# A two-layer model block on one core: experts taken in pairs in the column halves of TensorE, weights loaded in runs of 8 KB

## The chip, the core and the metric

The kernel runs on one core of one Trainium2 chip. A core has TensorE (PE in the profile, with PEld for its weight loads), VectorE (DVE), ScalarE (ACT), GpSimd (POOL) and SyncE (SP, whose queue starts nearly all DMA transfers of this kernel). The metric is the device time of one execution in microseconds; lower is better. Several executions are timed and the median is taken.

## What is computed

Two layers over 256 tokens of width 1024, each a mixer (retention and RWKV7), a cross-attention over a memory, and a grouped mixture of experts, with a layer norm behind each. The change touches the experts alone:

```python
def grouped_moe(x, router_w, router_bias, w_gate, w_up, w_down):
    ...
    y = jnp.zeros_like(t)
    for e in range(N_EXPERTS):
        h = jax.nn.silu(t @ w_gate[e]) * (t @ w_up[e])
        y = y + combine[:, e:e + 1] * (h @ w_down[e])
    return y.reshape(B, S, D)
```

There are 16 experts of width 512 in 4 groups; a token takes two experts of one group, so `combine` is zero for the other 14. Everything is fp32.

## The kernel before

**Which tokens an expert sees.** Each expert has a list of up to 64 tokens (`CAP`). `gather` (L1191) builds, for one group of four experts, the one-hot matrix `oh` of token against place in the list, and `columns` (L1199) multiplies the tokens with it: `xs` (the tokens as a high and a low part, tokens on the partitions, 1024 features in the row) is the operand that is loaded into the array as weights, 128 features at a time, and `oh` is streamed through with 256 columns. The result `xe` has features on the partitions and the 64 places of four experts in its columns. A layer has 128 such products. `columns` is a generator that `moe` moves on a step at a time between the products of the experts.

**The experts.** `moe` (L1106) goes through pairs of experts `p`. For each of the two experts, `expert_in` (L1238) makes the gate product, later the up product: the 64 columns of `xe` are the weights, a piece of the expert's matrix is streamed with 512 columns. 64 columns fill half of the array's 128 columns, so the even 128-row blocks of the contraction run in one column half and the odd ones in the other, side by side. The two partial sums then stand in different partitions of PSUM, and `halves` (L1249) adds them: ACT copies one half across (L1253, `low`), DVE adds the other (L1254). Silu is on ACT (L1150), the product of gate and up on DVE. `expert_mid` (L1256) transposes the result of both experts (four transposes, L131, in which `act` is the operand loaded as weights and the identity is streamed) and copies it from PSUM (`hT`, L1262). `expert_out` (L1265) makes the down product in the same way as the others, again with `halves` (`y`). `weighed` (L1276) multiplies with the combine weights and splits into `yh` (ACT, L1283) and `yl` (DVE, L1284), and `combine` (L1288) adds both to the output sums with eight full-width products (`y<-yh,ohT` and `y<-yl,ohT`), one pair later.

All products go through `mm`, so all of them have line L127 in the profile. One fp32 product of 64 columns by 512 is two instructions of the trace (written 128*64 there: 128 rows, 64 columns). The two column halves take instructions side by side when neighbours in PE's order lie in different halves.

**The weights.** 96 pieces of 1 MB a layer. `take` (L150 is the line of `fetch` that starts the transfer) asks for a piece on SP's queue and puts it into the next slot of a ring of 18 slots, which are buffers of several pools (`raw`, `wh`, `x`, `A` in the profile). A transfer waits until PE is through with the piece that had the slot before. `piece` (in the printed lines) gives a piece of 128 rows by k: each partition gets rows of the matrix that lie 128 rows apart, so runs of 2 KB in memory for gate and up (512 columns) and of 4 KB for down (1024 columns).

**What sets the order.** The code is written in the order of `moe`, and a scheduler orders each engine's instructions from it by when operands are ready and buffers come free; `behind` holds instructions back. PE runs its instructions strictly in the order that results.

Of the kernel before, what the change touches and what calls it, by code (L numbers as in the profile page):

```python
# [9 lines left out]
F32 = mybir.dt.float32  # L10
# [3 lines left out]
AF = mybir.ActivationFunctionType  # L14
# [6 lines left out]
D = 1024  # L21
# [4 lines left out]
FE = 512  # L26
# [89 lines left out]
class Build:  # L116
# [66 lines left out]
    @staticmethod  # L183
    def piece(w, k0, nk, c0, n):
        return w.rearrange("(k p) c -> p k c", p=128)[:, k0:k0 + nk, c0:c0 + n], [128, nk, n]

    @staticmethod
    def finish(steps):
# [917 lines left out]
    def moe(self, l, x, mem):  # L1106
        tc, nc, a, c = self.tc, self.nc, self.a, self.c
        wg, wu, wd = a["moe_w_gate"][l], a["moe_w_up"][l], a["moe_w_down"][l]
        py = [[self.pp.tile([128, 512], F32, name="y", tag="a", bufs=2) for _ in range(2)]]
        with ExitStack() as ctx:  # L1110
            mo = ctx.enter_context(tc.tile_pool(name="moe", bufs=1))
            with tc.tile_pool(name="route", bufs=1) as rp:
                rx = []
                for k in range(0, DK, 2):
                    ps = self.pp.tile([128, 2, 2, 128], F32, name="g", tag="b", bufs=4)
                    for j in range(2):
                        for tb in range(2):
# [12 lines left out]
            py.append([self.pp.tile([128, 512], F32, name="y", tag="c", bufs=2) for _ in range(2)])  # L1130
            for tb in range(2):
                for jc in range(2):
                    for i in range(2):
                        self.mm(py[tb][jc], self.identr, xs[i][:, tb, jc * 512:jc * 512 + 512], i == 0, False)
            lists, acts, ys = {}, {}, {}
            step = self.gather(mo, 0, xs, rank, cws, lists)
            self.finish(step)

            for p in range(NP + 2):
                if p < NP:  # L1140
                    if p % 2 == 0 and p < NP - 2:
                        step = self.gather(mo, p // 2 + 1, xs, rank, cws, lists)
                    xe = lists[p // 2][0]
                    act = mo.tile([128, 512], F32, name="act", bufs=2)
                    for o in range(2):
                        with self.behind(self.onehot) if p == 0 and o == 0 and NM > 0 else ExitStack():
                            ps = self.expert_in(wg[2 * p + o], [t[:, :, 2 * (p % 2) + o] for t in xe])
                        self.halves(mo, ps, act, o)
                        next(step, None)
                    nc.scalar.activation(act, act, AF.Silu)  # L1150
                    acts[p] = act
                if 1 <= p <= NP:
                    hT = self.expert_mid(mo, acts.pop(p - 1))
                if p < NP:
                    if p >= 2:
                        self.combine(p - 2, ys.pop(p - 2), lists[(p - 2) // 2][1][:, p % 2], py)
                    us = self.aux.tile([128, 512], F32, name="us", tag="sg", bufs=3)
                    for o in range(2):
                        ps = self.expert_in(wu[2 * p + o], [t[:, :, 2 * (p % 2) + o] for t in xe])
                        self.halves(mo, ps, us, o)  # L1160
                        next(step, None)
                    nc.vector.tensor_mul(out=act, in0=act, in1=us)
                    if p % 2:
                        self.finish(step)
                if 1 <= p <= NP:
                    y = [self.aux.tile([128, 512], F32, name="y", tag="sg", bufs=3) for _ in range(2)]
                    for o in range(2):
                        self.expert_out(mo, wd[2 * p - 2 + o], hT, y, o)
                        if p == NP and o == 0:
                            self.combine(p - 2, ys.pop(p - 2), lists[(p - 2) // 2][1][:, p % 2], py)  # L1170
                    ys[p - 1] = self.weighed(mo, y, lists[(p - 1) // 2][2][:, (p - 1) % 2:(p - 1) % 2 + 1])
                if p == NP + 1:
                    self.combine(p - 2, ys.pop(p - 2), lists[(p - 2) // 2][1][:, p % 2], py)
        self.extra.close()
        self.ring = [r for r in self.ring if r[1] == "raw2"]
        gb = self.norm(a["ln3_g"][l], a["ln3_b"][l])
        self.ring = [(self.wpool, "raw", self.nraw)] * self.nraw
        if l + 1 < self.layers:
            w = a["xa_wkv"][l + 1]
            self.prefetch([self.piece(w, hf * 4, 4, D + 512, 512) for hf in range(2)])  # L1180
        n = nc.values_load(flag[0:1, 0:1], min_val=0, max_val=2 * S)
        with tc.If(n > 0):
            self.overflow(l, xs, py, cover)
        x = self.xp.tile([128, 2, D], F32, name="x")

        self.layer_norm(lambda tb, j: py[tb][j], gb, x, LN_EPS / ALPHA ** 2)
        self.tail.close()
        self.tap("ln3", x)
        return x

    def gather(self, mo, g, xs, rank, cws, lists):  # L1191
# [5 lines left out]
        xe = []  # L1197

        def columns(k0):  # L1199
            t = mo.tile([128, 2, 4, 64], F32, name="xe", tag="xe", bufs=NXE)  # L1200
            ps = self.pp.tile([128, 2, 4, 64], F32, name="g", tag="b", bufs=4)
            for j in range(2):
                for i in range(2):
                    for tb in range(2):
                        k = k0 + j
                        self.mm(ps[:, j], xs[i][:, tb, k * 128:k * 128 + 128], oh[:, tb], j == 0 and tb == 0 and i == 0, tb == 1 and i == 1)
            if k0 % 4:
                nc.vector.tensor_copy(out=flat(t), in_=flat(ps))
            else:
                nc.scalar.copy(out=flat(t), in_=flat(ps))  # L1210
            xe.append(t)
# [23 lines left out]
            columns(k)  # L1235
        lists[g] = xe, ohT, ws

    def expert_in(self, w, xe):  # L1238

        ps = self.pp.tile([128, 512], F32, name="g", tag="b", bufs=4)  # L1240
        for hf in range(2):
            raw = self.take(*self.piece(w, hf * 4, 4, 0, FE))
            for k in range(0, 4, 2):
                t = xe[hf * 2 + k // 2]
                for j in range(2):
                    self.mm(ps[j * 64:j * 64 + 64, :], t[:, j], raw[:, k + j, :], hf == 0 and k == 0, hf == 1 and k == 2)
        return ps

    def halves(self, mo, ps, out, o):  # L1249

        h, x = slice(o * 64, o * 64 + 64), slice(64 - o * 64, 128 - o * 64)
        low = mo.tile([128, 512], F32, name="low", bufs=1)
        self.nc.scalar.copy(out=low[h], in_=ps[x])  # L1253
        self.nc.vector.tensor_add(out=out[h], in0=ps[h], in1=low[h])  # L1254

    def expert_mid(self, mo, g):  # L1256

        ps = self.pp.tile([128, 4, 128], F32, name="g", tag="b", bufs=4)
        for f in range(4):
            self.tr(ps[:, f, :], g[:, f * 128:f * 128 + 128])  # L1260
        hT = mo.tile([128, 4, 128], F32, name="hT", bufs=1)
        self.nc.vector.tensor_copy(out=flat(hT), in_=flat(ps))  # L1262
        return hT

    def expert_out(self, mo, wd, hT, y, o):  # L1265

        pd = [self.pp.tile([128, 512], F32, name="g", tag="b", bufs=4) for _ in range(2)]
        for hf in range(2):
            raw = self.take(*self.piece(wd, hf * 2, 2, 0, D))
            for jc in range(2):  # L1270
                for j in range(2):
                    self.mm(pd[jc][j * 64:j * 64 + 64, :], hT[:, hf * 2 + j, o * 64:o * 64 + 64], raw[:, j, jc * 512:jc * 512 + 512], hf == 0, hf == 1)
        for jc in range(2):
            self.halves(mo, pd[jc], y[jc], o)

    def weighed(self, mo, y, ws):  # L1276

# [94 lines left out]
```

## Time and profile before

| | |
|---|---|
| runs timed | 1318.68, 1309.84 and 1310.9 us, median 1310.9 |
| profiled execution | 1307.25 us, span 1305.5, granted clock 0.970 |
| PE | busy 1199.3 us, 92% of the span |
| DVE | busy 769.7 us, 59% |
| ACT | busy 500.1 us, 38% |
| DMA | 331.08 MB, 254 GB/s in the mean |

The share of an engine is its busy time over the whole span, which has stages of different kinds. A stage is read from the windows; a wait says which instruction was held up and by whom; the timeline gives start and length of instructions of one kind that stand behind each other. The expert stages lie at 451.4 to 675 us (layer 0) and 1073 to 1296 us (layer 1).

### The profile page before, as it was taken

To read this page: it belongs to the slowest core of one execution; us is meant where nothing else is said; L and a number is where in the kernel's file an instruction comes from. 1 tells how busy PE (TensorE), PEld (TensorE's weight loads), DVE (VectorE), ACT (ScalarE), POOL (GpSimd) and SP (SyncE) were. 2 spreads that over 40 slices of the span, in tenths; PEclk is the share of its full clock that TensorE was granted. 3 is DMA by queue.
4 is the path that set the end of the run, shared out by engine and by line. 5 is a ranking of instruction groups with operands and counts; after the bars stand their busy time and mean duration, and the time that the engine had idled before them with its cause. 6 is when DMAs were issued, how large, how long until landed. Compare 5 with 4: busy or idle time off the path is not lost. (4 is left out here: it accounts for less than half of the span.)

```text
span 1305.5 us, 19592 instructions
## 1 busy us (share of the span) xinstructions
PE 1199.3 (92%) x7648; PEld 850.1 (65%) x7648; DVE 769.7 (59%) x1574; ACT 500.1 (38%) x817; POOL 81.9 (6%) x157
## 2 busy tenths in 40 slices
PE   8999998998999999999969999989979969999995
PEld 7886787996988734433339876879959754433331
DVE  6589787777548423323356797876875562342335
ACT  4566433453544322322235664234534222232222
POOL 0022322000000000000000113220000000000000
PEclk9999989999999999999989999899989979999997
DMA  9746222298635899999986453131987249999994
GB/s 321 264 142 192 78 76 76 79 373 283 233 129 205 315 396 402 399 396 401 400 335 224 153 181 106 43 108 66 348 291 285 108 166 389 401 396 400 402 397 188
DMA packets 189842, 331.08 MB, mean 254 GB/s; under 512 B 23152, under 2 KB 80880, under 8 KB 188720
## 3 DMA queue, kind: packets, MB, share of 16 engines
q1 hardware_dynamic: 187728, 324.51, 69.0%
q10 hardware_dynamic: 1728, 3.15, 0.7%
q0 software_dynamic: 288, 2.10, 0.4%
q8 instruction: 64, 1.05, 0.3%
q14 instruction: 34, 0.28, 0.1%
HBM read 321.86 MB, written 7.87 MB: 253 GB/s over the span
## 5 line engine op out<-in xcount | busy, mean ns | idle before, releaser
L136 DVE TENSOR_TENSOR wh<-raw,wh 128x1024 fp32r<-128x1024 f32 (+1 forms) x204 | 233.3, 1147 | 122.8 <-ACT wh L135 121.4
L135 ACT CAST wh<-raw 128x1024 fp32r<-128x1024 f32 (+1 forms) x204 | 199.9, 981 | 181.8 <-PE acc L127 167.7
L127 PE MATMUL acc<-xT,wh 128*128 128x256 f32 x1824 | 246.0, 290 | 2.1 <-DVE xT L136 1.3
L127 PEld LDWEIGHTS acc<-xT,wh 128*128 128x128 f32 x1824 | 228.5, 193 | 6.5 <-issue 2.1
L1253 ACT COPY low<-g 64x512 f32<-64x512 f32 x128 | 74.2, 580 | 289.5 <-PE g L127 263.6
L127 PE MATMUL g<-raw,xe 128*64 128x512 f32 x688 | 157.7, 598 | 4.5 <-DVE hT L1262 3.5
L127 PEld LDWEIGHTS g<-raw,xe 128*64 128x64 f32 x688 | 46.0, 136 | 90.7 <-issue 80.2
L127 PE MATMUL acc<-wh,xT 128*128 128x512 f32 x384 | 99.8, 405 | 2.7 <-DVE vg L557 2.7
L1254 DVE TENSOR_TENSOR y<-g,low 64x512 f32<-64x512 f32 x64 | 44.1, 688 | 77.4 <-ACT low L1253 77.3
L127 PE MATMUL g<-raw,hT 128*64 128x512 f32 x352 | 81.4, 596 | 5.5 <-DVE y L1254 2.7
L127 PEld LDWEIGHTS acc<-wh,xT 128*128 128x128 f32 x384 | 70.2, 188 | 19.6 <-DVE vg L557 3.5
L1254 DVE TENSOR_TENSOR us<-g,low 64x512 f32<-64x512 f32 x32 | 22.0, 688 | 94.4 <-ACT low L1253 94.3
L1254 DVE TENSOR_TENSOR act<-g,low 64x512 f32<-64x512 f32 x32 | 22.0, 688 | 75.1 <-ACT low L1253 75.0
L127 PEld LDWEIGHTS g<-raw,hT 128*64 128x64 f32 x352 | 26.0, 137 | 55.0 <-issue 41.9
L127 PE MATMUL acc<-wh,memT 128*128 128x512 f32 x192 | 50.7, 415 | 0.3 <-ACT memT L135 0.3
L127 PE MATMUL acc<-memT,wh 128*128 128x256 f32 x384 | 46.7, 283 | 1.1 <-DVE wh L136 0.7
L127 PEld LDWEIGHTS acc<-memT,wh 128*128 128x128 f32 x384 | 46.1, 190 | 1.8 <-DVE wh L136 0.9
L127 PE MATMUL acc<-wh,mT 128*128 128x512 f32 x192 | 45.9, 397 | 0.7 <-DVE xr L406 0.7
L127 PE MATMUL acc<-wh,oT 128*128 128x512 f32 x192 | 45.6, 394 | 1.0 <-DVE x L406 0.8
L127 PE MATMUL acc<-ys,wh 128*128 128x256 f32 x384 | 45.6, 280 | 0.0
L127 PEld LDWEIGHTS acc<-ys,wh 128*128 128x128 f32 x384 | 45.4, 188 | 0.0
L127 PEld LDWEIGHTS g<-oh,xs 128*128 128x128 f32 x256 | 33.5, 196 | 17.1 <-issue 11.2
(296 smaller groups left out, 1684.5 us busy)
## 6 DMA issues: line engine op xcount, KB each, us to landing
raw<-in_w_in_dram SPq DMA_DIRECT2D x46, 1024.0 KB, 5.2
raw<-in_moe_w_down_dram SPq DMA_DIRECT2D x44, 1024.0 KB, 14.9
raw<-in_moe_w_gate_dram SPq DMA_DIRECT2D x43, 1024.0 KB, 14.0
raw<-in_moe_w_up_dram SPq DMA_DIRECT2D x43, 1024.0 KB, 13.8
raw<-in_xa_wkv_dram SPq DMA_DIRECT2D x16, 1024.0 KB, 10.1
wh<-in_moe_w_up_dram SPq DMA_DIRECT2D x15, 1024.0 KB, 14.2
A<-in_moe_w_down_dram SPq DMA_DIRECT2D x10, 1024.0 KB, 13.7
A<-in_moe_w_gate_dram SPq DMA_DIRECT2D x9, 1024.0 KB, 13.7
```

The source lines that it names most:

```text
L127: self.nc.tensor.matmul(out, lhsT, rhs, start=start, stop=stop, skip_group_check=True)
L135: self.nc.scalar.copy(out=hi, in_=src)
L136: (eng or self.nc.vector).tensor_sub(out=lo, in0=src, in1=hi)
L1253: self.nc.scalar.copy(out=low[h], in_=ps[x])
L1254: self.nc.vector.tensor_add(out=out[h], in0=ps[h], in1=low[h])
```

## The change

The two experts of a pair take the two column halves, instead of the even and odd blocks of one expert. Each half then holds a finished sum, so `halves` is no longer there; Silu, the product of gate and up, and `weighed` read the sums from PSUM. `expert_in` and `expert_out` become `experts_in` and `experts_out`, which take a piece of each of the two experts and alternate between them.

A piece now holds the same megabyte in another shape: `together` gives each partition rows that lie next to each other, 8 KB in one run, four rows of gate and up or two of down. So partition p holds rows 4p to 4p+3 of a half of the matrix (2p and 2p+1 for down), and the other operand must have its contraction in the same order: `columns` loads `xs` into the array with a step of four columns, `expert_mid` loads `act` with a step of two. The number of products, transposes, transfers and their bytes, and the order of pieces and slots on SP's queue, are the same.

```diff
+    def together(w, hf):
+        n = w.shape[0] // 256
+        return w.rearrange("(h p k) c -> h p k c", h=2, k=n)[hf], [128, n, w.shape[1]]
...
+                    with self.behind(self.onehot) if p == 0 and NM > 0 else ExitStack():
+                        ps = self.experts_in(wg, p, xe)
                     act = mo.tile([128, 512], F32, name="act", bufs=2)
-                    for o in range(2):
-                        with self.behind(self.onehot) if p == 0 and o == 0 and NM > 0 else ExitStack():
-                            ps = self.expert_in(wg[2 * p + o], [t[:, :, 2 * (p % 2) + o] for t in xe])
-                        self.halves(mo, ps, act, o)
-                        next(step, None)
-                    nc.scalar.activation(act, act, AF.Silu)
+                    nc.scalar.activation(act, ps, AF.Silu)
...
-                        self.mm(ps[:, j], xs[i][:, tb, k * 128:k * 128 + 128], oh[:, tb], j == 0 and tb == 0 and i == 0, tb == 1 and i == 1)
+                        c0 = k // 4 * 512
+                        self.mm(ps[:, j], xs[i][:, tb, c0 + k % 4:c0 + 512:4], oh[:, tb], j == 0 and tb == 0 and i == 0, tb == 1 and i == 1)
...
+    def experts_in(self, w, p, xe):
         ps = self.pp.tile([128, 512], F32, name="g", tag="b", bufs=4)
         for hf in range(2):
+            raw = [self.take(*self.together(w[2 * p + o], hf)) for o in range(2)]
+            for k in range(4):
                 t = xe[hf * 2 + k // 2]
+                for o in range(2):
+                    self.mm(ps[o * 64:o * 64 + 64, :], t[:, k % 2, 2 * (p % 2) + o], raw[o][:, k, :], hf == 0 and k == 0, hf == 1 and k == 3)
...
-    def halves(self, mo, ps, out, o):
-        h, x = slice(o * 64, o * 64 + 64), slice(64 - o * 64, 128 - o * 64)
-        low = mo.tile([128, 512], F32, name="low", bufs=1)
-        self.nc.scalar.copy(out=low[h], in_=ps[x])
-        self.nc.vector.tensor_add(out=out[h], in0=ps[h], in1=low[h])
...
-            self.tr(ps[:, f, :], g[:, f * 128:f * 128 + 128])
+            c0 = f // 2 * 256
+            self.tr(ps[:, f, :], g[:, c0 + f % 2:c0 + 256:2])
...
+    def experts_out(self, wd, p, hT):
         pd = [self.pp.tile([128, 512], F32, name="g", tag="b", bufs=4) for _ in range(2)]
         for hf in range(2):
+            raw = [self.take(*self.together(wd[2 * p + o], hf)) for o in range(2)]
             for jc in range(2):
                 for j in range(2):
+                    for o in range(2):
+                        self.mm(pd[jc][o * 64:o * 64 + 64, :], hT[:, hf * 2 + j, o * 64:o * 64 + 64], raw[o][:, j, jc * 512:jc * 512 + 512],
+                                hf == 0 and j == 0, hf == 1 and j == 1)
```

The gathers move on at other places too: both steps of a pair's gate come behind it, and both of an even pair's up.

PE's order changes with it. The first place is a late pair of layer 0, from its down products to the next pair's gate. Before (`raw`, `wh`, `x` and `A` are weight pieces; the rows with `hT` are down products, those with `xe` gate or up products, `g<-cst,act` the transposes, `y<-...` the products of `combine`):

```order
L127 MATMUL g<-raw,hT 64x512 x4
L127 MATMUL g<-raw_5526,hT 64x512 x4
L127 MATMUL g<-wh,hT 64x512 x8
L127 MATMUL g<-wh,xe 64x512 x4
L127 MATMUL y<-yh,ohT 128x512
L127 MATMUL y<-yl,ohT 128x512
...
L127 MATMUL g<-x,xe 64x512 x4
L127 MATMUL y<-yl,ohT 128x512
L127 MATMUL g<-A,xe 64x512 x4
L131 MATMUL g<-cst,act 128x128 x4
L127 MATMUL g<-A,xe 64x512 x4
```

The same place in the change, where `raw` and `raw_5366` are the pieces of the pair's two experts, each in its own column half:

```order
L127 MATMUL g<-raw,hT 64x512 x2
L127 MATMUL g<-raw_5366,hT 64x512
L127 MATMUL g<-raw,hT 64x512
L127 MATMUL g<-raw_5366,hT 64x512 x2
L127 MATMUL g<-raw,hT 64x512
L127 MATMUL g<-raw_5366,hT 64x512
L127 MATMUL g<-wh,hT 64x512 x8
L127 MATMUL y<-yh,ohT 128x512 x2
L127 MATMUL y<-yl,ohT 128x512 x2
L127 MATMUL y<-yh,ohT 128x512
L127 MATMUL g<-wh,xe 64x512
L131 MATMUL g<-cst,act 128x128 x4
```

The down products went from four of one expert after four of the other to two, one, one, two, one, one; combine stands directly behind them; and a single gate product stands ahead of the four transposes, where a group of four stood.

The second place is ACT's order in the middle of layer 0 (`low` is the copy of a half, `act<-` Silu, `yh` the weighing, `xe<-g` a copy of the gather). Before:

```order
L1210 COPY xe<-g 128x512
L1253 COPY low<-g 64x512 x2
L1150 ACTIVATE act<-act 128x512
L1253 COPY low<-g 64x512 x6
L1283 ACTIVATE yh<-y,ws 128x512 x2
```

In the change:

```order
L1153 ACTIVATE act<-g 128x512
L1216 COPY xe<-g 128x512
L1284 ACTIVATE yh<-g,ws 128x512 x2
L1153 ACTIVATE act<-g 128x512
L1227 CAST ohT<-g 128x512
```

The eight copies of a pair are no longer there, and Silu and the weighing take `g`, a bank of PSUM, as their operand.

## Rows read from the trace of the kernel before

**Rows 1.** The page's 40 slices: busy tenths of the DMA engines.

```profile
DMA  9746222298635899999986453131987249999994
```

**Rows 2.** Windows: length, busy us of PE PEld DVE ACT POOL, clock, DMA share, GB/s.

```profile
451.40:675.00 223.60, 212.07 (x1021) 83.23 (x1020) 77.18 (x113) 63.26 (x101) 0.00 (x0) 0.99 1.02 394
1073.00:1296.00 223.00, 210.71 (x1021) 82.73 (x1020) 78.38 (x119) 60.25 (x98) 0.00 (x0) 0.99 0.97 372
1060.00:1100.00 40.00, 35.14 (x210) 19.27 (x211) 12.56 (x38) 8.11 (x14) 0.00 (x0) 0.91 0.79 293
```

**Rows 3.** PE's waits at 451.4 to 675 us: total us, times, longest.

```profile
PE g L127 <- DVE hT L1262: 3.4, 4, 1.3
PE g L127 <- DVE y L1254: 3.0, 6, 0.5
PE y L127 <- ACT yh L1283: 2.4, 3, 2.0
PE y L127 <- DVE yl L1284: 0.6, 2, 0.3
...
PE g L127 <- DMA raw<-in_moe_w_down_dram: 0.2, 1, 0.2
```

**Rows 4.** Waits of SP's DMA queue at 400 to 720 us.

```profile
SPq L150 <- PE g L127: 119.9, 62, 7.9
```

**Rows 5.** PE's waits at 1073 to 1296 us, where they differ from rows 3.

```profile
PE g L127 <- DVE y L1254: 2.5, 5, 0.5
```

**Rows 6.** Timeline of PE: start us, us, engine, line, op, tiles, shape, count.

```profile
451.42 3.65 PE L127 MATMUL g<-raw,xe 128*64 128x512 f32 x16
...
471.57 1.03 PE L127 MATMUL g<-raw,xe 128*64 128x512 f32 x4
472.53 2.15 PE L127 MATMUL g<-oh,xs 128*128 128x256 f32 x16
474.62 2.79 PE L127 MATMUL g<-raw,xe 128*64 128x512 f32 x12
...
513.20 3.94 PE L127 MATMUL g<-raw,hT 128*64 128x512 f32 x16
517.67 4.18 PE L127 MATMUL g<-wh,hT 128*64 128x512 f32 x16 [0.53 <-DVE y L1254]
...
615.94 1.03 PE L127 MATMUL g<-A,xe 128*64 128x512 f32 x4
616.80 7.04 PE L127 MATMUL g<-raw,xe 128*64 128x512 f32 x32
623.66 7.04 PE L127 MATMUL g<-raw,hT 128*64 128x512 f32 x32
```

**Rows 7.** Timeline of PE behind the last down product of layer 0.

```profile
670.05 1.14 PE L127 MATMUL y<-yh,ohT 128*128 128x512 f32 x2 [1.96 <-ACT yh L1283]
```

**Rows 8.** Groups by line and shape, ACT: busy us, mean ns, idle before.

```profile
L1283 ACT ACTIVATE yh<-y,ws 128x512 fp32r<-128x512 f32 x32 | 23.1, 722 | 0.7
```

**Rows 9.** Groups by line and shape, PE's weight loads, 440 to 660 us.

```profile
L127 PEld LDWEIGHTS g<-oh,xs 128*128 128x128 f32 x128 | 16.1, 188 | 8.6 <-issue 6.0 <-DVE yl L1284 0.8 <-DVE ws L1231 0.8
```

**Rows 10.** Groups by line and shape, DVE in the mixer, whole span.

```profile
L812 DVE TENSOR_TENSOR blkT<-blkO,blkM 64x225 f32<-64x225 f32 x4 | 2.1, 534 | 0.1
...
L814 DVE TENSOR_REDUCE blkO<-blkT 64x15 f32<-64x225 f32 x4 | 1.5, 374 | 0.1
...
L812 DVE TENSOR_TENSOR blkT<-blkO,blkM 64x64 f32<-64x64 f32 x4 | 1.0, 255 | 0.1
...
L814 DVE TENSOR_REDUCE blkO<-blkT 64x8 f32<-64x64 f32 x4 | 0.8, 212 | 0.1
```

**Rows 11.** Windows by the runs that move: 2 KB, 4 KB, mixed with 8 KB.

```profile
624.00:642.00 18.00, 17.47 (x80) 6.18 (x78) 7.00 (x10) 5.03 (x9) 0.00 (x0) 1.00 1.05 389
1228.00:1240.00 12.00, 11.47 (x50) 4.30 (x50) 4.09 (x6) 3.07 (x5) 0.00 (x0) 1.00 1.03 416
...
692.80:695.40 2.60, 2.60 (x17) 2.18 (x16) 2.24 (x5) 1.51 (x3) 0.00 (x0) 1.00 1.01 353
```

More of the change, by code (lines that the diff above doesn't have):

```diff
@@ L185, in piece @@
         return w.rearrange("(k p) c -> p k c", p=128)[:, k0:k0 + nk, c0:c0 + n], [128, nk, n]
+    @staticmethod
+    def together(w, hf):
+        n = w.shape[0] // 256
+        return w.rearrange("(h p k) c -> h p k c", h=2, k=n)[hf], [128, n, w.shape[1]]
     @staticmethod
@@ L1143, in moe @@
                     xe = lists[p // 2][0]
+                    with self.behind(self.onehot) if p == 0 and NM > 0 else ExitStack():
+                        ps = self.experts_in(wg, p, xe)
                     act = mo.tile([128, 512], F32, name="act", bufs=2)
-                    for o in range(2):
-                        with self.behind(self.onehot) if p == 0 and o == 0 and NM > 0 else ExitStack():
-                            ps = self.expert_in(wg[2 * p + o], [t[:, :, 2 * (p % 2) + o] for t in xe])
-                        self.halves(mo, ps, act, o)
-                        next(step, None)
-                    nc.scalar.activation(act, act, AF.Silu)
+                    nc.scalar.activation(act, ps, AF.Silu)
                     acts[p] = act
+                    if p % 2 == 0:
+                        for _ in range(2):
+                            next(step, None)
                 if 1 <= p <= NP:
@@ L1156, in moe @@
                         self.combine(p - 2, ys.pop(p - 2), lists[(p - 2) // 2][1][:, p % 2], py)
[L1157 to L1162, printed above, removed]
+                    ps = self.experts_in(wu, p, xe)
+                    nc.vector.tensor_mul(out=act, in0=act, in1=ps)
                     if p % 2:
                         self.finish(step)
+                    else:
+                        for _ in range(2):
+                            next(step, None)
                 if 1 <= p <= NP:
[L1166 to L1171, printed above, removed]
+                    pd = self.experts_out(wd, p - 1, hT)
+                    if p == NP:
+                        self.combine(p - 2, ys.pop(p - 2), lists[(p - 2) // 2][1][:, p % 2], py)
+                    ys[p - 1] = self.weighed(mo, pd, lists[(p - 1) // 2][2][:, (p - 1) % 2:(p - 1) % 2 + 1])
                 if p == NP + 1:
@@ L1236, in gather @@
         lists[g] = xe, ohT, ws
-    def expert_in(self, w, xe):
+    def experts_in(self, w, p, xe):
         ps = self.pp.tile([128, 512], F32, name="g", tag="b", bufs=4)
         for hf in range(2):
-            raw = self.take(*self.piece(w, hf * 4, 4, 0, FE))
-            for k in range(0, 4, 2):
+            raw = [self.take(*self.together(w[2 * p + o], hf)) for o in range(2)]
+            for k in range(4):
                 t = xe[hf * 2 + k // 2]
-                for j in range(2):
-                    self.mm(ps[j * 64:j * 64 + 64, :], t[:, j], raw[:, k + j, :], hf == 0 and k == 0, hf == 1 and k == 2)
-        return ps
-    def halves(self, mo, ps, out, o):
-        h, x = slice(o * 64, o * 64 + 64), slice(64 - o * 64, 128 - o * 64)
-        low = mo.tile([128, 512], F32, name="low", bufs=1)
-        self.nc.scalar.copy(out=low[h], in_=ps[x])
-        self.nc.vector.tensor_add(out=out[h], in0=ps[h], in1=low[h])
+                for o in range(2):
+                    self.mm(ps[o * 64:o * 64 + 64, :], t[:, k % 2, 2 * (p % 2) + o], raw[o][:, k, :], hf == 0 and k == 0, hf == 1 and k == 3)
+        return ps
     def expert_mid(self, mo, g):
@@ L1263, in expert_mid @@
         return hT
-    def expert_out(self, mo, wd, hT, y, o):
+    def experts_out(self, wd, p, hT):
         pd = [self.pp.tile([128, 512], F32, name="g", tag="b", bufs=4) for _ in range(2)]
         for hf in range(2):
-            raw = self.take(*self.piece(wd, hf * 2, 2, 0, D))
+            raw = [self.take(*self.together(wd[2 * p + o], hf)) for o in range(2)]
             for jc in range(2):
                 for j in range(2):
-                    self.mm(pd[jc][j * 64:j * 64 + 64, :], hT[:, hf * 2 + j, o * 64:o * 64 + 64], raw[:, j, jc * 512:jc * 512 + 512], hf == 0, hf == 1)
-        for jc in range(2):
-            self.halves(mo, pd[jc], y[jc], o)
+                    for o in range(2):
+                        self.mm(pd[jc][o * 64:o * 64 + 64, :], hT[:, hf * 2 + j, o * 64:o * 64 + 64], raw[o][:, j, jc * 512:jc * 512 + 512],
+                                hf == 0 and j == 0, hf == 1 and j == 1)
+        return pd
     def weighed(self, mo, y, ws):
```

## The prediction

> **What bounds the kernel now.** I read the slices of the page first, for the stage that the change touches: a slice is 32.6 us, and in slices 15 to 20 and 34 to 39, from 457 and 1077 us on, the DMA engines are full [rows 1]. These are the expert stages of the two layers. The windows over them give numbers: 223.6 and 223.0 us, in which PE is busy 212.1 and 210.7 us at a granted clock of 0.99, while the DMA engines have a share of 1.02 and 0.97 [rows 2]. DVE (77 us) and ACT (63 us) are far from full.
>
> So there are two candidates, and the waits tell them apart. In the stage of layer 0 PE waits for a weight piece once, for 0.2 us; what it waits for otherwise is DVE and ACT: the copy of hT, the sum of the two halves (y), and yh and yl behind it [rows 3]. The DMA queue on its side waits 119.9 us for PE to give slots back [rows 4]. PE therefore ends the stage, and DMA only just keeps up: that one wait of 0.2 us says that the margin is small.
>
> **What the change removes.** `halves` goes, with its ACT copy and DVE sum, and with it most of PE's waits: hT waits because the sums stand ahead of it on DVE, y is the sum itself, and yh and yl stand behind it. In layer 0 the four rows make 9.4 us in 15 waits; in layer 1 three of these rows come back with the same numbers and y is 2.5 in 5, 8.9 us in 14 [rows 3, 5]. A wait costs more than its idle time. A block of 32 half-width instructions is 7.04 us long, but the next starts 6.86 us after it: 0.18 us of each block lies under the next one, where nothing is waited for [rows 6]. Where PE waits that overlap is lost. So 18.3 + 29 x 0.18 = 23.5 us. One wait stays: behind the last down product PE waits 1.96 us for yh, and after the change yh alone, 0.72 us, still lies between [rows 7, 8]; 2 x 0.7 = 1.4. **Removed: 22.1 us.** The freed time of ACT and DVE is worth nothing by itself, since both engines are far from full [rows 2].
>
> **What the change does to PE's order.** Number and form of the products stay. Their price is read from the slot: 16 products, 32 instructions, half of them in each column half, start 6.86 us apart, so 0.43 us per product when the halves alternate [rows 6]. A product that stands alone, or the odd one at the end of a block, leaves the other half idle for 0.43 us. Three things differ in the order:
>
> (1) From the third pair on, a single gate product is set before the four transposes, and gathers cut blocks at odd places. I counted, block by block between two full-width instructions, the difference between the halves: none before, 16 slots in layer 0 and 18 in layer 1 after. 34 x 0.43 = **+14.6 us**.
>
> (2) The down products no longer alternate, but go A A B A B B A B (the two experts of the pair). Two neighbours of the same half stand in each eight: 42 such neighbours over both layers against 8 before. The few blocks that already run so in before are 3.94 and 4.18 us long, where a regular block of the same 16 instructions takes 3.65 [rows 6]: 0.29 and 0.53 more, for two neighbours each, about 0.2 per neighbour. 34 x 0.2 = **+6.8 us**.
>
> (3) Changes from column halves to the full array and back: 45 each way instead of 55. Out of a half-width block of four the next start is 0.96 us off, against 0.86 where another half-width block follows [rows 6]: 0.1 us, and I take the same for the way back, which no row isolates. 10 x 0.2 = **-2.0 us**.
>
> **The stepped reads.** The gather's weight load now takes 128 columns of xs with a step of four fp32 values, so 16 bytes from one to the next. No PE read in the trace of before has a step, so its price has to be bounded. Below: nothing, if the load (188 ns recorded [rows 9]) stays under the products: 16 gather products take 2.09 us with the change of width, 0.12 to 0.13 us each [rows 6]. Above: the load grows as DVE's reads do. On DVE, the product whose one operand is read with an inner step of 16 fp32 goes from 255 ns at 64 elements to 534 at 225, 1.73 ns an element; the sum over contiguous elements goes from 212 to 374, 1.01 ns [rows 10]. A load that grew in that ratio from its recorded 188 ns would be 322, 0.20 us more than now's spacing per product, +46 us over 224 gather products at full clock (the 32 in layer 1 that run at the lower level, in a stretch with a mean clock of 0.91 [rows 2], hide more of it). Between the two I take the reading that needs no ratio: one column of the load per 1.73 ns as DVE's stepped operand, 128 x 1.73 = 221 ns, against a spacing of about 0.12: 0.10 us each, 224 x 0.10 = **+23 us**. This is the term that decides, and it is an estimate from another engine.
>
> [...]
>
> The transposes load act with a step of two (8 bytes). Bounds: nothing, and 64 transposes by 0.08 us, half of what DVE's step adds, +5 us. [...] The one-hot, the weighing and combine keep their instructions. DVE's product reads PSUM where it read SBUF; the cover for it is the down block of the pair before, 3.4 to 6.9 us of PE work, and without that cover it would stand in PE's way as y's sum does now, 0.5 us at a time [rows 3].
>
> **The transfers.** 8 KB per partition and run instead of 2 KB (gate, up) and 4 KB (down). Where 2 KB rows alone move, 389 GB/s at a share of 1.05; 4 KB rows, 416 at 1.03; in a short mixed stretch with 8 KB runs 353 at 1.01 [rows 11]. Taken per share: 370, 404, 350. The order of the pieces and of the ring's slots is the same. Since PE ends the stage, faster transfers bring **nothing** by themselves; they only let DMA follow if PE gets faster. Bounds: the 4 KB rate for all, which takes about 9 us a layer off the transfers of gate and up (two thirds of 224 us by 34/404, and part of it lies ahead of the stage), and 353 GB/s, a loss (last rival).
>
> **Sum.** 1307.25 (the profiled execution, span 1305.5) - 22.1 - 2.0 + 14.6 + 6.8 + 23 = 1327.6. The median of the three runs, 1310.9, is 3.65 above that execution, so the forecast for the median is 1331, 1.5% more.
>
> **The rivals.**
> - *The weight load hides its step* (no penalty, or one that stays under the 0.12 us of its product). For it: loads overlap products, and 0.12 is all that they show per gather product [rows 6]. Against: DVE's rows [rows 10]. Time: 1331 - 23 = 1308, no change: waits won and order lost cancel. A penalty of half the size gives 1320. [...]
> - *The load is hidden and the order costs little*, since the queue starts a product of the other half earlier than I count: the other side. The price of (1) rests on counting, not on a row. If at most half of the 21.4 us comes, 1297; if none, 1287. It decides from about 11 us of order losses downwards. It needs DMA to follow by 10 us a layer, which the 4 KB rate just allows.
> - *The load costs by DVE's ratio*: +46 in place of +23, 1354.
> - *8 KB runs move like the mixed stretch*, 353 GB/s: 394 x 223.6 us is 88 MB, which takes 250 us, and DMA becomes the bound, 26 us a layer: 1310.9 + 52 = 1363. Against it: the step from 2 to 4 KB made transfers faster, and that stretch holds few transfers of several kinds.
>
> **How the numbers follow.** Full step price as in the sum: 0.45. Half of it, 1320: 0.12. Hidden load with the order losses, 1308: 0.22. Hidden load and few order losses, 1287 to 1297: 0.15. Worse than the sum, 1354 and 1363: 0.06. The likeliest is 1331; the terms of order and waits, each good to a third, give it 1320 to 1342 by itself. The range from 1295 to 1342 leaves out the two high cases and most of the lowest. About 1% (13 us) can be told from no change: below 1298 is the third rival, 0.15; above 1324 is nine tenths of the first case and the high ones, 0.41 + 0.06 = 0.47; the rest, 0.38, lies between.
>
> **What would show it.** In the changed trace: the loads g<-oh,xs recorded well above 188 ns and 16 gather products over 3.5 us instead of 2.1 confirm the step; 2.1 us refutes it, and the time falls to 1308 or lower. Waits of PE for DVE and ACT in the stages under 3 us a layer confirm the first term. A down block of 16 instructions near 4.05 us and a single gate product that takes 0.86 before the transposes confirm the order terms. PE waits for raw<-in_moe_... of more than a few us would say that DMA has become the bound, and that the forecast was built on the wrong engine.

## The result, and the profile after

The changed kernel takes 1330.4 us in the median of 4 runs (1328.1 to 1337.0), the kernel before 1310.4. The ratio is 1.0144, with a 95% interval of 1.0114 to 1.0174: slower, by 20 us. The forecast was 1331. The total came out; two of its terms did not, and they cancelled, as the experiments show.

The page of the changed kernel, total of TensorE, and the slices of DMA (busy tenths, then GB/s):

```profile
PE 1237.1 (93%) x7648; PEld 886.2 (67%) x7648; DVE 680.7 (51%) x1446; ACT 424.4 (32%) x689; POOL 81.9 (6%) x157
...
DMA  9746222398636899999936363222986249999990
GB/s 316 267 147 188 65 75 74 121 365 293 206 127 227 319 410 423 423 422 421 411 137 215 129 187 97 67 82 91 362 294 238 96 185 410 423 422 422 422 379 33
```

PE has 38 us more to do, with the same number of instructions, while DVE and ACT have 89 and 76 us less. The transfers of the expert stages run at about 422 GB/s. The slice behind each full stretch, the 21st and the 40th, falls to 3 and 0 tenths, where it was 8 and 4 before [rows 1]: DMA is through before PE is.

The windows over the two expert stages, from the first gate product to the last product of `combine` (columns as in [rows 2]):

```profile
454.51:680.16 225.65, 224.80 (x1021) 96.26 (x1020) 30.58 (x46) 22.77 (x36) 0.00 (x0) 1.00 0.92 381
1086.42:1312.57 226.15, 225.30 (x1021) 96.46 (x1020) 30.36 (x46) 21.17 (x34) 0.00 (x0) 1.00 0.88 367
```

From the first gate product to the end, the stages of before are 222.3 and 219.9 us long by the same reading of the timeline. PE now idles under 1 us in each stage. All its waits in the stage of layer 0, where [rows 3] has five lines and more:

```profile
PE g L127 <- DVE act L1165: 0.8, 1, 0.8
```

So the waits went as forecast, and PE is slower all the same: it does the same instructions more slowly. Where, the timeline of PE shows (start, length, count):

```profile
450.57 4.01 PE L127 MATMUL g<-oh,xs 128*128 128x256 f32 x16
454.51 7.09 PE L127 MATMUL g<-raw,xe 128*64 128x512 f32 x32
...
523.95 3.60 PE L127 MATMUL g<-wh,hT 128*64 128x512 f32 x16
...
641.79 1.07 PE L127 MATMUL g<-raw,xe 128*64 128x512 f32 x2
642.80 0.74 PE L131 MATMUL g<-cst,act 128*128 128x128 f32 x4
...
670.78 7.08 PE L127 MATMUL g<-raw,hT 128*64 128x512 f32 x28
677.79 0.73 PE L127 MATMUL y<-yh,ohT 128*128 128x512 f32 x2
```

Sixteen gather products take 3.94 us from start to start, where they took 2.09 [rows 6]. A down block of 16 instructions takes 3.60, no longer than a regular one. One gate product alone holds PE for 1.01 us, with the change of width. The last block of 28 would need 6.0 us if the halves were equal (an estimate, 14 slots of 0.43 us), and takes 7.01; and `combine` follows it with no wait, where PE waited 1.96 us before [rows 7].

The weight loads, by line and shape, over the whole span ([rows 9] has the gather's of before):

```profile
L127 PEld LDWEIGHTS g<-oh,xs 128*128 128x128 f32 x256 | 61.4, 329 | 11.5 <-issue 10.5 <-PE g L127 0.8
...
L131 PEld LDWEIGHTS g<-cst,act 128*128 128x128 f32 x64 | 8.9, 207 | 9.8 <-issue 6.5 <-DVE act L1165 1.7 <-DVE ws L1237 1.6
```

The stepped load of gather is recorded with 329 ns for 188; the transposes' load, with a step of two, with 207, where versions without that step have 140.

### The profile page after: what moved, and what is told of

Its sections match the earlier page's. It is cut to its first block, busy times and chain, and to the rows that moved or that the text cites. A ratio compares the mean times of both kernels' runs of the same rounds, so it can differ in the third digit from the quotient of the medians.

```text
span 1325.7 us, 19215 instructions
## 1 busy us (share of the span) xinstructions
PE 1237.1 (93%) x7648; PEld 886.2 (67%) x7648; DVE 680.7 (51%) x1446; ACT 424.4 (32%) x689; POOL 81.9 (6%) x157
## 5 line engine op out<-in xcount | busy, mean ns | idle before, releaser
L127 PE MATMUL g<-raw,xe 128*64 128x512 f32 x688 | 176.5, 596 | 0.0
L127 PE MATMUL g<-raw,hT 128*64 128x512 f32 x352 | 95.3, 594 | 0.0
L1165 DVE TENSOR_TENSOR act<-act,g 128x512 f32<-128x512 f32 x16 | 11.0, 687 | 150.8 <-PE g L127 150.8
L1284 ACT ACTIVATE yh<-g,ws 128x512 fp32r<-128x512 f32 x32 | 22.0, 688 | 191.7 <-PE g L127 191.7
L1285 DVE SCALAR_TENSOR_TENSOR yl<-g,ws,yh 128x512 fp32r<-128x512 f32 x32 | 24.0, 751 | 109.2 <-ACT yh L1284 108.0
L127 PEld LDWEIGHTS g<-oh,xs 128*128 128x128 f32 x256 | 61.4, 329 | 11.5 <-issue 10.5
L1214 DVE COPY xe<-g 128x512 f32<-128x512 f32 x16 | 11.1, 692 | 111.0 <-PE g L127 111.0
L127 PE MATMUL g<-oh,xs 128*128 128x256 f32 x256 | 64.9, 409 | 0.0
L127 PEld LDWEIGHTS g<-raw,hT 128*64 128x64 f32 x352 | 30.2, 137 | 50.4 <-issue 49.5
L127 PE MATMUL g<-wh,xe 128*64 128x512 f32 x184 | 55.7, 595 | 0.0
L1153 ACT ACTIVATE act<-g 128x512 f32<-128x512 f32 x16 | 9.6, 598 | 129.0 <-PE g L127 129.0
## 6 DMA issues: line engine op xcount, KB each, us to landing
raw<-in_xa_wkv_dram SPq DMA_DIRECT2D x16, 1024.0 KB, 10.3
A<-in_moe_w_gate_dram SPq DMA_DIRECT2D x9, 1024.0 KB, 11.3
```

What stands on the lines that cost most here:

```text
L127: self.nc.tensor.matmul(out, lhsT, rhs, start=start, stop=stop, skip_group_check=True)
L1153: nc.scalar.activation(act, ps, AF.Silu)
L1165: nc.vector.tensor_mul(out=act, in0=act, in1=ps)
L1284: nc.scalar.activation(yh, y[jc], AF.Copy, scale=ws)
L1285: nc.vector.scalar_tensor_tensor(out=yl, in0=y[jc], scalar=ws, in1=yh, op0=OP.mult, op1=OP.subtract)
```

## The experiments

**The step, taken out of the change.** The gather's load in the changed kernel:

```diff
-                        c0 = k // 4 * 512
-                        self.mm(ps[:, j], xs[i][:, tb, c0 + k % 4:c0 + 512:4], oh[:, tb], j == 0 and tb == 0 and i == 0, tb == 1 and i == 1)
+                        self.mm(ps[:, j], xs[i][:, tb, k * 128:k * 128 + 128], oh[:, tb], j == 0 and tb == 0 and i == 0, tb == 1 and i == 1)
```

> The changed kernel with one edit: gather loads 128 neighbouring columns of xs as weights again, without the step of four. PE's order, the transfers and the other step stay. The features then stand in another order than the weight rows, so the output isn't the reference's; the work and its order are the same. Theory (the step costs PE time in every gather product): in the changed kernel gather products start 0.234 us apart, before 0.118; 224 at full clock make 26 us, and the 32 ahead of layer 1's stage about 1 more. The time goes from 1330 to 1303, the recorded load from 329 to 188 ns, 16 gather products take 2.1 us. Rival (the order of PE's products is what costs, and the longer load lies beside them): 1322 or more.

Measured: 1302.0 us, ratio to the kernel before 0.9917 (0.9880 to 0.9953). Without the step the change would have been a gain of 10 us. The step costs 28.3 us by the medians of the two kernels, which were timed in different sets, and 30.2 if each is taken against the kernel before in its own set. The rival that put the loss into the order falls.

**The step, put into the kernel before.** The same edit the other way round.

> The kernel before with one edit: gather loads its 128 columns of xs with a step of four. Nothing else changes, so the features stand in another order than the weight rows and the output isn't the reference's. Theory (the step costs by itself, and PE ends the expert stages there too): gather products 0.234 us apart in place of 0.118, about 27 us more, 1334 to 1339. Rival (part of it is hidden, because a later PE finds its operands ready and its waits shrink by as much): the waits of PE in the stages, 10.3 and 8.9 us before, fall by some us, and the time is 1325 to 1332.

Measured: 1338.6, ratio 1.0214 (1.0176 to 1.0252), 27.9 us more than before on that chip. The two measurements of the step agree within some 2 us, so nothing else in the change hides or worsens it by more than that. The rival's part did not come: PE still waits 9.4 us in the stage of layer 0, where it waited 10.3, and 8.9 in layer 1, as before. The step's full price arrives.

**Which steps cost.** In the kernel before, the groups of experts are gathered with steps of 8, 2, 3 and 6:

```diff
-                        self.mm(ps[:, j], xs[i][:, tb, k * 128:k * 128 + 128], oh[:, tb], j == 0 and tb == 0 and i == 0, tb == 1 and i == 1)
+                        st = (8, 2, 3, 6)[g]
+                        c0 = k if st > 4 else k * 32
+                        self.mm(ps[:, j], xs[i][:, tb, c0:c0 + 127 * st + 1:st], oh[:, tb], j == 0 and tb == 0 and i == 0, tb == 1 and i == 1)
```

> The kernel before with another step in each group's gather: 8 fp32 values in the first group of a layer, then 2, 3 and 6. It measures the load alone; the features gathered are not the right ones, so the output isn't the reference's. Theory (what counts is how many values come from each 16 bytes): 6 and 8 cost what 4 costs, loads recorded near 329 ns and products 0.234 us apart; 2 costs nothing, 188 ns and 0.118; 3, where four values come from three lines on average, lies between, nearer to 4. Rival (the price grows with the distance): 8 about twice the price of 4, 6 half as much again, 3 three quarters, 2 half.

One execution, 1324.9 us. The timeline of PE, blocks of gather products with a step of 8, 2, 3 and 6, each with the block behind it:

```profile
452.02 4.14 PE L127 MATMUL g<-oh,xs 128*128 128x256 f32 x16
456.08 3.65 PE L127 MATMUL g<-raw,xe 128*64 128x512 f32 x16
...
464.41 1.23 PE L127 MATMUL g<-oh,xs 128*128 128x256 f32 x8
465.57 3.65 PE L127 MATMUL g<-raw,xe 128*64 128x512 f32 x16
...
501.69 1.68 PE L127 MATMUL g<-oh,xs 128*128 128x256 f32 x8
503.30 3.65 PE L127 MATMUL g<-raw,xe 128*64 128x512 f32 x16
...
556.92 2.07 PE L127 MATMUL g<-oh,xs 128*128 128x256 f32 x8
558.83 0.39 PE L127 MATMUL y<-yh,ohT 128*128 128x512 f32 x1
```

The median distance between the starts of neighbouring gather products, over both layers' groups at full clock, from the same timeline:

| step in fp32 values | 1 | 2 | 3 | 4 | 6 | 8 |
|---|---|---|---|---|---|---|
| us between starts | 0.118 | 0.120 | 0.175 | 0.234 | 0.227 | 0.242 |
| stretches of 16 bytes touched per value | 0.25 | 0.5 | 0.75 | 1 | 1 | 1 |

(Steps 1 and 4 are from the kernel before and the changed one.) Distance is not what costs: 6 and 8 cost within 4% of what 4 costs (0.227 and 0.242 us, for 0.234). The number of 16-byte stretches that the load touches fits all six steps: from 4 values on, 16 bytes apart, the distance stays at 0.227 to 0.242 us, and 3 values, 12 bytes, cost three quarters of what 4 cost. 128 stretches take 0.234, 96 take 0.175, in the ratio of 4 to 3, or 1.83 ns a stretch; 64 at that pace would take 0.117, an estimate, and products without a step start 0.118 apart, so a step of two is free here, at 0.120. A step of four fp32 values is not: 0.234 us, 0.118 without.

**The loads alone.** The kernel before, with `together` in place of `piece` in `expert_in` and `expert_out`, and no step anywhere.

> The kernel before with its pieces loaded in runs of 8 KB per partition and nothing else changed; the order of rows isn't matched in gather and transposes, so the output isn't the reference's. Theory (PE ends the expert stages): transfers rise from about 398 to 422 GB/s as in the changed kernel, SP waits longer for slots, and the time stays at 1307 to 1312. Rival (DMA holds part of the stage, as the small lead of the pieces suggests): 1300 or less.

Measured: 1309.5, ratio 0.9997 (0.9973 to 1.0020). The slices of GB/s show the faster transfers:

```profile
GB/s 322 265 143 190 77 75 76 66 373 279 249 125 201 319 421 423 423 421 421 422 195 217 160 181 106 43 108 65 342 289 288 112 167 407 423 422 422 423 421 51
```

About 422 in place of 398, and no time: PE ends the stage, as read from [rows 3, 4]. (The total wait of SP's queue for PE did not grow, it is 100.6 us; part of its waits are now put down to transfers. That part of the expectation missed.)

**The pairing alone.** The changed kernel with the old pieces and contiguous reads:

```diff
-            raw = [self.take(*self.together(w[2 * p + o], hf)) for o in range(2)]
+            raw = [self.take(*self.piece(w[2 * p + o], hf * 4, 4, 0, FE)) for o in range(2)]
...
```

> The changed kernel with the pieces of the kernel before (runs of 2 KB for gate and up, 4 KB for down) and no step in any load: only the pairing of experts in the column halves and its order stay. Theory (2 KB runs fed PE only just before, so a PE that is 10 us per layer faster now waits for DMA): PE waits for raw<-in_moe_ several us in each stage, time 1305 to 1311, no gain on the kernel before. Rival (DMA still keeps up): no such waits, 1302, as with 4 KB runs.

Measured: 1314.9, ratio 1.0010 (0.9986 to 1.0034), 4 us above the expectation. PE's waits for DMA in the stage of layer 0:

```profile
PE g L127 <- DMA wh<-in_moe_w_up_dram: 1.6, 1, 1.6
PE g L127 <- DMA x<-in_moe_w_up_dram: 1.4, 1, 1.4
PE g L127 <- DMA raw<-in_moe_w_down_dram: 1.0, 2, 0.6
```

Neither edit gains anything alone. With pairs PE would be 8 us faster in layer 0 and 5 in layer 1 (the stages of the next version against those of before), and then transfers of 2 KB runs, about 400 GB/s, no longer keep up: the window of the stage is 221.9 us long, 7.8 more than with the next version.

**Pairs, 4 KB runs, a step of two.** Gate and up come as two runs of two neighbouring rows, so gather steps by two; down comes in its old pieces, so the transposes have no step:

```diff
+        return w.rearrange("(h q p k) c -> h p q k c", h=2, q=2, k=2)[hf], [128, 2, 2, w.shape[1]]
...
+                        c0 = k // 2 * 256
+                        self.mm(ps[:, j], xs[i][:, tb, c0 + k % 2:c0 + 256:2], oh[:, tb], j == 0 and tb == 0 and i == 0, tb == 1 and i == 1)
...
```

> The changed kernel with other pieces: gate and up in two runs of 4 KB per partition (two neighbouring rows of 2 KB in each quarter of the matrix), down as before the change; gather's load has a step of two, the transposes none. PE's order is that of the changed kernel, row for row. Theory (a step costs only when each value comes from another 16 bytes; with two values from each it is free): gather products 0.12 to 0.13 us apart, time 1302 to 1306. Rival (the price grows with the step): half the price, 0.17 to 0.18 apart, 1315 to 1318. The transposes' recorded load goes from 207 back to 140 ns.

Measured: 1298.3, ratio 0.9909 (0.9874 to 0.9943), a few us under the expectation. In a second set on another chip:

> The version with separate pieces in 4 KB runs and a step of two once more, beside the next run on the same chip, with more rounds: its stages are 214.1 and 214.6 us long in the trace and its median was 1298.3. Expected 1297 to 1300.

1302.0, ratio 0.9931 (0.9907 to 0.9955), a little above it. Taken together some 0.8% faster than before. This is the change without its dear step. Its order on PE is that of the changed kernel, row for row, so its stages show what the order costs. Those of the second set (in the first they were 214.1 and 214.6 us long):

```profile
453.03:667.02 213.99, 213.14 (x1021) 84.55 (x1020) 30.59 (x46) 23.67 (x36) 0.00 (x0) 1.00 1.02 408
1071.51:1286.09 214.58, 213.72 (x1021) 84.77 (x1020) 30.39 (x46) 21.36 (x34) 0.00 (x0) 1.00 0.96 387
```

**The order, mended in the pieces.** One piece holds a quarter of both experts' matrices, so both halves' products become ready together and the scheduler has no reason to take one without the other:

```diff
+        return w.rearrange("e (q p k) c -> q p e k c", q=4, k=k)[q], [128, 2, k, w.shape[2]]
...
+        for q in range(4):
+            raw = self.take(*self.together(w[2 * p:2 * p + 2], q, 2))
+            for k in range(2):
+                for o in range(2):
+                    self.mm(ps[o * 64:o * 64 + 64, :], xe[q][:, k, 2 * (p % 2) + o], raw[:, o, k, :], q == 0 and k == 0, q == 3 and k == 1)
...
```

Unequal halves fall from 16 and 18 slots a layer to none, neighbours in one half from 22 and 20 to none.

> A version of the change in which one piece holds a quarter of the matrices of both experts of a pair: runs of 4 KB, gather's load with a step of two, no step in the transposes. Both halves' products then become ready together, and PE's order has no single gate product ahead of the transposes and no neighbours in one half: everything stands in fours that alternate. Theory (the order of the changed kernel costs about 8.5 us per layer over the slot price of 0.43 us, read from the summed starts of its half-width products): time 1284 to 1290 if the 4 KB runs keep up, half-width products at their slot price, and DMA waits as the next bound. Rival (the order is free, the halves catch up): the same as with separate pieces of 4 KB runs, 1302 to 1306.

Measured: 1297.9, ratio 0.9889 (0.9853 to 0.9925), above the expectation and no better than separate pieces beside it. Yet the stages were shorter. So both were timed again:

> The version with shared pieces once more. Its two stages were 212.0 and 209.0 us long, 7.7 us shorter together than with separate pieces, but the median was only 0.5 us lower. Theory (the rest of the program took the gain in that one execution, by a lower clock in the mixers, and not always): 1291 to 1295 in the median. Rival (what follows a stage does not start when it ends: the loads of the memory come late behind it whatever the stage does): again within 2 us of the separate pieces.

Measured: 1294.1, ratio 0.9862 (0.9839 to 0.9885), 7.9 us below separate pieces in the same set. Its stages:

```profile
454.65:666.72 212.07, 208.92 (x1021) 80.96 (x1020) 29.79 (x45) 22.09 (x34) 0.00 (x0) 1.00 1.03 412
1069.56:1278.85 209.29, 207.82 (x1021) 81.24 (x1020) 30.25 (x46) 21.97 (x34) 0.00 (x0) 1.00 0.99 397
```

They are 7.2 us shorter than the two of the separate pieces, close to what the medians of this set differ by. In layer 0 PE waits 2.5 us for down pieces: DMA begins to be the next bound. This version is the best of the study, 1.4% faster than the kernel before. In the first set the gain did not arrive: layer 1's stage began 5.3 us later there than with separate pieces; the starts of PE's instructions fall behind at several places in the mixer, and 2.1 us of it lie in the gather just ahead of the stage, at a granted clock of 0.50 in place of 0.70 (last section). Why the rest fell behind in that set was not settled.

**Prices in the order, one at a time.** First the down products, held in strict turns by an order on PE alone (`behind`), on the version with separate pieces:

> The version with separate pieces in 4 KB runs and a step of two, with the down products held in strict turns between the two halves by an order on PE alone. Of the order's faults, counted in the code, neighbours in one half fall from 42 to 0 and the difference between the halves from 34 slots to 26. By the prediction's prices (0.2 us a neighbour, 0.43 us a slot) the half-width products of the two stages, 176.4 and 177.2 us there, would take 170.3 and 171.5, and the time be about 1286. By the version with shared pieces, which has neither fault and took 172.4 and 170.2 with DMA waits in them, a neighbour costs only some 0.05 us: 173.5 and 174.5, time about 1293.

Its windows over the two stages:

```profile
455.82:669.03 213.21, 212.14 (x1021) 84.74 (x1020) 30.05 (x45) 22.81 (x35) 0.00 (x0) 1.00 1.02 410
1070.64:1282.40 211.76, 211.76 (x1021) 85.21 (x1020) 30.36 (x46) 22.08 (x34) 0.00 (x0) 1.00 0.98 392
```

3.7 us less than separate pieces in the first set (214.1 and 214.6), with 1.1 us of new waits for DMA in layer 0 against it. The 8 slots fewer make 3.4. And a wait of 0.8 to 0.9 us for DVE's product of gate and up, which separate pieces have once in each layer, is no longer there. The two together are all of it, so nothing is left for 42 neighbours. The half-width products took 175.9 us, waits included, and 174.4, nowhere near the prediction's price. The median, 1298.3, lies above both expectations and shows no gain over the first set of separate pieces.

Then the single gate product, which the transposes can't pass before four have gone:

> The version with separate pieces, with the transposes held on PE behind the first four gate products of the next pair, so that no single product stands ahead of them. The scheduler then cuts other blocks: counted in the code, the difference between the halves grows from 16 and 18 slots to 20 and 22, with 27 blocks a layer for 24. By the slot price of 0.43 us and 0.1 us more per block each way the half-width products and the changes take about 2 us a layer more than 176.4 and 177.2. If unequal halves cost nothing, they take the same or less.

One execution, 1305.0 us. Its windows over the two stages:

```profile
453.45:670.37 216.92, 216.07 (x1021) 85.45 (x1020) 30.66 (x46) 23.66 (x36) 0.00 (x0) 1.00 1.01 403
1072.16:1289.66 217.50, 216.65 (x1021) 85.73 (x1020) 30.36 (x46) 22.08 (x34) 0.00 (x0) 1.00 0.95 382
```

The half-width products take 178.6 and 179.3 us (summed from each start to the next), 2.2 and 2.1 more, where four slots and three blocks make 2.0. Unequal halves cost what the slot says. The traces allow the count itself to be tested: instructions that share a slot start 0.01 us apart. Counted by these starts, the half-width products of a layer take 16 and 18 slots more than an even split would in the changed kernel and in the version with separate pieces, 20 and 22 here, and none with shared pieces. That is the count of the unequal halves alone; the neighbours add no slot to it.

## Why the prediction was right, and which steps of it were not

- **What bounds the stage: right.** Faster transfers alone brought nothing (0.9997), and PE's waits are what fell. That the margin of DMA is small was right as well: with pairs and the old pieces PE waits for DMA and the gain is gone.
- **The stepped load: right in kind, 23 us forecast, 28 to 30 measured** (28.3 or 30.2 taken out, 27.9 put in). The price per product was 0.116 us, not 0.10, so 26 us at full clock. The 32 products ahead of layer 1's stage, which the forecast left out, cost 0.8 us: at a granted clock of 0.50 they start 0.239 us apart with the step and 0.21 without (10.0 us for 9.2, last section). Over both layers the gathers and the stretches ahead of the stages take 26.5 us more in the changed kernel's trace than in that of the version without the step. The estimate came from DVE's 1.73 ns per stepped element; the load's own figure is 1.83 ns per 16-byte stretch (0.234 us for 128). That the two are close is luck: no run ties DVE's read to the load's. What the load followed in the sweep is the number of such stretches, 0.175 us for 96 and 0.227 to 0.242 for 128, which the DVE row alone could not tell.
- **The waits: right, 22.1 us forecast, about 23 measured.** 10.3 and 8.9 us in 32 times fell to 0.8 and 0.8 us in two; with 0.18 for each of 30, 23.0. The two that are left are for DVE's product of gate and up, which the forecast had named as a risk. The 1.4 us that it kept for the wait ahead of the last `combine` went too.
- **(1) Unequal halves, +14.6: right.** The trace shows the 16 and 18 slots that were counted. 1.01 us for a product alone, and 2.2 and 2.1 us for four more slots and three blocks, agree with 0.43 us a slot. Without any unequal halves the half-width products took 172.5 and 170.4 us in place of 176.4 and 177.2: 3.9 less in layer 0 and 6.8 in layer 1, where 16 and 18 slots make 6.9 and 7.7. Both figures have other things in them: new waits, 2.8 us in layer 0 and 1.2 in layer 1, and a wait for DVE of 0.8 us in each layer that went. (The stages gained less, 7.2 us, since `combine` took some 1.5 us a layer more in that order.)
- **(2) Neighbours in one half, +6.8: wrong, nothing to be seen.** This is the step that failed. The two irregular blocks of [rows 6], 3.94 and 4.18 us, were taken as the price of their order. In the changed kernel a down block of 16 instructions takes 3.60 us, and strict turns gave nothing beyond the slots and the wait they saved. What made the two blocks long is in the trace of before. In the middle of each, one half stands still until a sum of `halves` ends on DVE, at 514.29 and 519.00 us, and its next weight load follows 0.06 us later:

```profile
513.60 0.69 DVE L1254 TENSOR_TENSOR us<-g,low 64x512 f32<-64x512 f32 x1 [3.43 <-ACT low L1253]
...
514.35 0.13 PEld L127 LDWEIGHTS g<-raw,hT 128*64 128x64 f32 x1
...
518.32 0.68 DVE L1254 TENSOR_TENSOR y<-g,low 64x512 f32<-64x512 f32 x1 [0.70 <-ACT low L1253]
...
519.06 0.20 PEld L127 LDWEIGHTS g<-wh,hT 128*64 128x64 f32 x3 [0.34 <-DVE y L1254]
```

The profile names DVE's sum as what the second load waited for; for the first, the same distance is the evidence, and layer 1 has the same pair at 1135.88 and 1140.58 us. A down product doesn't read that sum; by the code it can only wait for the bank of PSUM that the sum had still to read. PE was busy in the other half meanwhile, so that PE's list of waits [rows 3] has neither. The 0.29 and 0.53 us were thus waits that the change removes, some 1.6 us over both layers, and the forecast counted them as a price that it adds.
- **(3) Changes of width, -2.0: right in kind.** In the traces PE leaves half-width blocks 24 times a layer, for 31 and 30 before; at 0.2 us for both ways -2.6.
- **The transposes, without a term in the sum: about 1.3 us.** From each start to the next they take 4.4 and 4.2 us a stage with the step of two, 3.7 and 3.5 in the version without it; they start 0.120 us apart in place of 0.109. So the step of two, free in the gather, whose products start 0.118 us apart without it, is not free here: 64 stretches at 1.83 ns make 0.117 us, an estimate that lies above 0.109.
- **The sum.** All but the step was forecast at -2.7 us and measured at -10.2 (the change without its step against before). The corrections above, -6.8 and -1.6 for (2), -0.9, -0.6 and +1.3, give -11.3. In the traces the two stages are 12.7 us shorter (214.5 and 215.0 us), and the gather ahead of layer 1's stage is 2.7 longer, at a granted clock of 0.50 in place of 0.76, which comes and goes between executions of one program (last section). The step was 5 to 7 us dearer than forecast. So the forecast hit by two misses of about 5 to 7 and 7.5 us that go against each other. That is luck, for which its range of 47 us had room.
- **The rivals.** The hidden load: refuted, it was not hidden. Its number, 1308, would have been 1302, as the change without the step shows. The cheap order: right for the neighbours, wrong for the slots. The load by DVE's ratio, and 8 KB runs at 353 GB/s, did not come: 422.

## What to carry to other kernels

A layout that makes a transfer's runs longer may be paid for where the other operand is read: before taking it, find out what the step costs there. Here it was TensorE's weight load, and its price followed the stretches of 16 bytes that it touches: the step that left two fp32 values in each was nearly free (gather products 0.120 us apart for 0.118), and the one that left a single value (0.234) cost 28 to 30 us. Ask as well which bound the edit moves; here two edits that were each worth nothing alone gave 0.8% together, because each held the other up. And where two halves of the array run side by side, give them operands that arrive together, since a product that goes alone costs a slot (0.43 us here). A price read from two odd blocks of a trace should not be used without asking what else is odd about them: PE's list of waits is blind to one half that waits while the other works, but the timeline of its weight loads showed it.

## What the runs showed of the hardware

The first gather of layer 1 stands behind waits of PE (4.4 and 1.5 us), and all or part of it runs at a granted clock of 0.50, where the changed kernel's expert stages run at 1.00. The windows over it, in this order, in the kernel before, the changed kernel, the change without the step of four, and the version with a step of two in its first and second set:

```profile
1066.40:1072.90 6.50, 6.50 (x54) 6.24 (x52) 1.00 (x3) 1.76 (x3) 0.00 (x0) 0.76 0.10 42
```

```profile
1076.40:1086.40 10.00, 10.00 (x54) 9.42 (x53) 1.00 (x3) 2.92 (x4) 0.00 (x0) 0.50 0.04 15
```

```profile
1062.92:1072.15 9.23, 9.23 (x54) 8.66 (x52) 1.00 (x3) 2.75 (x4) 0.00 (x0) 0.50 0.02 5
```

```profile
1061.00:1068.20 7.20, 7.20 (x54) 6.85 (x54) 1.00 (x3) 1.94 (x4) 0.00 (x0) 0.69 0.09 36
1062.28:1071.51 9.23, 9.23 (x55) 8.66 (x53) 1.00 (x3) 2.76 (x4) 0.00 (x0) 0.50 0.02 8
```

At a clock of 0.50, gather products without a step or with a step of two start 0.21 us apart, not quite twice the 0.118 to 0.120 at 1.00; those with a step of four 0.239, against 0.234, so half the clock hardly changed their distance. At a clock of 0.50 throughout, the step of four makes the stretch 10.0 us long in place of 9.2.

PE is busy throughout in all five windows; the clock stays at 0.50 in three, and in two it rises on the way, to 0.76 and 0.69 in the mean. The step is not what decides it. The same program with a step of two shows both, the change without any step stays low, and in the kernel before a step of four stays at 0.51 and a step of 8 rises to 0.77 in the mean. What does decide it was not found. It is worth up to 2.7 us in a run, since the transposes of the one-hot and the products behind them also run at 0.50: in the changed kernel the transposes start 0.21 us apart there, 0.109 at 1.00.

The transfers of the weights ran at about 400, 413 and 422 GB/s in the full slices, with 2 KB (down 4 KB), 4 KB and 8 KB per run.
